# A two-layer trunk whose first projection takes its inputs in another order: loads of both token halves in one transfer, memory keys block by block, and the memory's scale factor spread later

## The chip, the core and the metric

The kernel runs on one core of a Trainium2 chip. The engines spoken of are TensorE (PE: matrix products, with weight loads listed apart as PEld), VectorE (DVE), ScalarE (ACT), GpSimd (POOL) and SyncE (SP, which here only issues transfers). The metric is the device time of one execution in microseconds (us), as the median of several runs.

## The reference

What is computed is a trunk of two layers of width 2048 for 256 tokens, each layer with a mixer, an attention into 256 memory tokens and a gated feed-forward part. All inputs are float32. Cut to what matters here (the mixers and the feed-forward part are left in words, since the change lies ahead of them):

```python
def rmsnorm(x, g):
    y = x * rsqrt(mean(x * x, axis=-1, keepdims=True) + EPS)
    return y * g

def memory_attention(q_m, mem, g_mem, w_mem_kv):       # 4 heads of 128
    q = q_m.reshape(B, S, 4, 128)
    kv = rmsnorm(mem, g_mem) @ w_mem_kv                # (256 x 2048) @ (2048 x 1024)
    k, v = kv[..., :512] , kv[..., 512:]               # each as (B, 256, 4, 128)
    s = einsum('bshd,bmhd->bhsm', q, k) * 128 ** -0.5
    return einsum('bhsm,bmhd->bshd', softmax(s), v).reshape(B, S, 512)

for l in range(2):
    h = rmsnorm(x, g_mix[l])
    if l == 0: main, q_m = spatial gating of h @ w_in_a
    else:      main, q_m = latent attention of h @ w_in_b over keys from layer 0's result
    mo = memory_attention(q_m, mem, g_mem[l], w_mem_kv[l])
    x = x + concatenate([main, mo]) @ w_out[l]
    x = x + conv_ffn(rmsnorm(x, g_ffn[l]), w_ffn_up[l], conv_w[l], conv_b[l], w_ffn_down[l])
return rmsnorm(x, g_final)
```

The memory's keys and values of both layers depend on `mem`, `g_mem` and `w_mem_kv` alone, not on `x`. So the kernel can compute them first, while `x` is still on its way.

## The kernel before, in words

**Products.** Partitions are P = 128 rows; D = 2048 is NB = 16 blocks of 128. A float32 product is made of three products of reduced operands: each operand is split into a high part and a low part, and the kernel adds hi x hi, hi x lo and lo x hi. `chunk` (L98) loads two blocks of weights, 128 x 1024 elements (512 KB), into a tile `raw` of which there are four. Where a norm's gain has to be applied (it does for the memory's weights), ACT writes `whi` for each block as a scaled copy (L121) and DVE writes `wlo`, the scaled weights less `whi` (L122). `whi` and `wlo` have five tiles each.

`gemm_fm` (L161) leaves the features of the result on the partitions; its inner loop `mm_fm` (L152) runs, for a chunk of two input blocks and four output blocks, first all products with `whi` (L155 with the operand's high part, L156 with its low part, alternating), then all with `wlo` (L158), 24 products of 256 columns. `gemm_tm` (L199) leaves the tokens on the partitions (L193 to L195, 512 columns each). Four accumulators in PSUM stay open over all 16 input blocks.

**The start.** `start` (L433) makes, in this order, the memory's keys of layer 0 (`gemm_fm`), its values (`gemm_tm`), the keys of layer 1 and the values of layer 1. The memory tokens come as they lie, a token on a partition, in two tiles `mtok` of 128 tokens each, and must be transposed: `token_transpose` (L398) puts two blocks of both halves through PE (L403, four transposes, one group in what follows), then `put_mem` (L449) has ACT write the high part `memhl` (L452) and DVE the low part (L453). `token_load` (L393) loads a range of columns, with one transfer for each half. `gains` (L315) loads rows of gains, transposes them on PE (L327) and has DVE copy them to `gT` (L328); without `gT` no memory weight can be split.

`begin` (L487) holds what comes ahead of the first product. It spreads the first transfers over the queues of ACT and SP: quarters of the first four blocks of tokens (128 rows x 256 columns each), the weights of blocks 0 and 1 as two halves of one `raw`, and the gains. Between, `idle` (L481) lets PE multiply ones by ones, 11 times in all, the results of which nothing reads. Token blocks 0 and 1 are transposed before `gemm_fm` is entered, blocks 2 and 3 after the first chunk's split.

**What sets the order.** The keys of layer 0 stand in a region in which the order on ACT, DVE, PE and SP is the order of the program (`manual_schedule`). There `gemm_fm` splits chunk n+1 before it multiplies chunk n (L176 to L183), and the hooks in `first` put, after the products of chunk c, the transposes of blocks 2c+4 and 2c+5 and the loads of the later tokens. What follows the region is put in order by a scheduler; the program gives it hooks too, which run after a given chunk. In the hooks of the layer-0 values stand the loads of x, the memory's squares on ACT (L412), their sums, and in the one of chunk 5 `scale_keys` (L469). `scale_keys` spreads the memory's factor, 1/rms of each memory token, over all partitions: `spread` (L423) has DVE multiply the identity by the factor (`diag`, L428) and PE multiply ones by it (L429), once for each half; ACT copies the sum, and POOL multiplies layer 0's four key tiles by it (L472). The keys of layer 1 are multiplied by the same spread factor when they are evicted.

Of the kernel before, what the change touches and what calls it, by code (L numbers as in the profile page):

```python
# [69 lines left out]
class Kernel:  # L70
# [27 lines left out]
    def chunk(self, src, nk, ncol, gains=None, heads=None, raw=None, moves=False):  # L98
        nc, n = self.nc, nk * ncol
        loaded = raw is not None  # L100
        if not loaded:
            raw = self.wp.tile([P, 1024], F32, tag="raw", name=self.uid("raw"), bufs=4)
        hi, lo = self.split_tile("whi", moves), self.split_tile("wlo", moves)
        view = lambda x: x[:, :n].rearrange("p (k c) -> p k c", k=nk)
        if not loaded:
            nc.sync.dma_start(out=view(raw), in_=src)
# [54 lines left out]
    def gemm_fm(self, src, kbs, nblk, rhs, evict, nk=2, gain=None, hooks={}, raw=None):  # L161
# [3 lines left out]
        def split(c):  # L165
            g = None if gain is None else [gain(kbs[c + i]) for i in range(nk)]
            hi, lo = self.chunk(src(kbs[c], nk), nk, nblk * P, g, raw=raw if c == 0 else None)
# [8 lines left out]
        ready = []  # L176
        for n, c in enumerate(chunks):
            ahead = chunks[n : n + 2] if raw is not None else [c]
            for d in ahead[len(ready) :]:
                ready.append(split(d))  # L180
                for f in hooks.get(-1, ()) if d == 0 else ():
                    f()
            self.mm_fm(ready.pop(0))  # L183
            for f in hooks.get(n, ()):
                f()
# [207 lines left out]
    def token_load(self, src, tok, k0, k1):  # L393
        c = slice(k0 * P, k1 * P)
        for tb in range(2):
            self.nc.sync.dma_start(out=tok[tb][:, c], in_=src[tb * P : (tb + 1) * P, c])

    def token_transpose(self, tok, k0, k1, put):  # L398
        for k in range(k0, k1, 2):
            acc = self.psum()  # L400
            for i in range(2):
                for tb in range(2):
                    self.nc.tensor.transpose(  # L403
                        acc[:, i * S + tb * P : i * S + (tb + 1) * P], tok[tb][:, (k + i) * P : (k + i + 1) * P], self.ident
                    )
# [3 lines left out]
    def token_squares(self, tok, part, j, pool):  # L409
        for tb in range(2):  # L410
            junk = self.tmp(pool, [P, 512], "junk", 2)
            ins = self.nc.scalar.activation(  # L412
                junk, tok[tb][:, j * 512 : (j + 1) * 512], AF.Square, accum_out=part[:, tb, j : j + 1]
# [19 lines left out]
    def start(self):  # L433
# [8 lines left out]
        with tc.tile_pool(name="st", bufs=1) as st:  # L442
            self.gp = st
            mtok = [st.tile([P, D], F32, name=f"mtok{tb}") for tb in range(2)]
            xtok = [st.tile([P, D], F32, name=f"xtok{tb}") for tb in range(2)]
# [28 lines left out]
            raw = self.wp.tile([P, 1024], F32, tag="raw", name=self.uid("raw"), bufs=4)  # L474
            first = {c: [mturn(2 * c + 4, 2 * c + 6)] for c in range(-1, 6)}
            first[-1].append(lambda: idle(1))
            for c, piece in ((0, (4, 6)), (1, (6, 8)), (2, (8, 12)), (4, (12, 16))):
                first[c].insert(0, mload(*piece))


# [618 lines left out]
```

## Time and profile before

| | |
|---|---|
| median of 3 runs | 2065.43 us (2065.27 to 2065.58) |
| the profiled execution | 2065.32 us |
| its span in the profile | 2063.6 us |
| PE busy in the span | 2053.1 us (99%) |
| ACT busy | 1074.8 us (52%) |
| DVE busy | 1376.3 us (67%) |
| moved by DMA | 392.56 MB, mean 190 GB/s |
| first product of the keys of layer 0 | at 8.63 us |
| first product of the values of layer 0 | at 34.17 us |

The profile is one execution. Times in its rows count from the start of the span; the execution's time includes about 1.7 us around it. A row of the timeline names the start, the duration, the engine, the line of the kernel, the operation and its tiles (written <- read), and in brackets the idle time before it with what ended it. The waits view sums idle time by the instruction that waited and what released it. Matmuls overlap, so two rows that start 0.114 us apart may each be listed with 0.28 us; what PE takes is read from the distance of starts.

### The profile page before, as it was taken

The numbers are of one execution on the slowest core, as the hardware profiler recorded it, in microseconds if no ns is written. First come the engines' busy times: TensorE is split into PE (matmuls) and PEld (weight loads), VectorE is DVE, ScalarE is ACT, GpSimd is POOL, SyncE is SP. The second block draws the span as 40 slices with busy tenths as digits, with TensorE's granted clock in tenths as the row PEclk, the third lists the DMA queues.
The fourth block names the chain that finished last, engine by engine and source line by source line (L and its number), as shares of the span: only waits on it lengthen the run. The fifth ranks groups of instructions, "written<-read, shape, count | busy, mean of one in ns | idle before, by whom it ended". The sixth has DMA issues, their size and how long they took to land.

```text
span 2063.6 us, 39742 instructions
## 1 busy us (share of the span) xinstructions
PE 2053.1 (99%) x16322; PEld 1984.5 (96%) x16322; DVE 1376.3 (67%) x2051; ACT 1074.8 (52%) x1536; POOL 141.2 (7%) x200
## 2 busy tenths in 40 slices
PE   9999999999999999999999999999999999999998
PEld 9889999999999999999999999999988999889996
DVE  5656666776656767557788676776765677646765
ACT  6754644555534555345555574455543555435554
POOL 0000012100000000000043241400000000000000
PEclk9999999999999999999999999999999999999999
DMA  8665556566556665566555634565655666556654
GB/s 271 207 214 174 163 186 200 187 197 193 195 194 194 194 194 194 194 194 195 194 194 175 184 122 165 184 204 181 192 191 193 196 197 194 191 194 195 195 183 143
DMA packets 208122, 392.56 MB, mean 190 GB/s; under 512 B 14334, under 2 KB 23876, under 8 KB 207812
## 3 DMA queue, kind: packets, MB, share of 16 engines
q1 hardware_dynamic: 207364, 388.98, 58.2%
q8 instruction: 127, 2.08, 0.4%
q10 hardware_dynamic: 576, 1.05, 0.2%
q14 instruction: 55, 0.45, 0.1%
HBM read 387.88 MB, written 2.10 MB: 189 GB/s over the span
## 4 chain that ended last, share of the span: by engine, by line
PE 97%; DMA 1%; ACT 1%; DVE 0%; issue 0%; SPq 0%; ACTq 0%; DVEq 0%
PE ps L155 26%; PE ps L156 26%; PE ps L158 26%; PE ps L193 6%; PE ps L194 6%; PE ps L195 6%; DMA raw<-in_w_mem_kv 1%; ACT whi L121 0%; PE ps L918 0%; PE ps L919 0%; PE ps L581 0%; PE ps L546 0%; DMA xtok<-in_x 0%; PE ps L729 0%; PE ps L952 0%
## 5 line engine op out<-in xcount | busy, mean ns | idle before, releaser
L117 DVE TENSOR_TENSOR wlo<-raw,whi 128x1024 fp32r<-128x1024 f32 x660 | 818.6, 1243 | 543.9 <-ACT whi L116 537.6
L116 ACT ACTIVATE whi<-raw 128x1024 fp32r<-128x1024 f32 x660 | 701.1, 1063 | 868.1 <-PE ps L156 664.7
L155 PE MATMUL ps<-xhl,whi 128*128 128x256 f32 x3264 | 764.6, 277 | 0.0
L156 PE MATMUL ps<-xhl,whi 128*128 128x256 f32 x3264 | 761.1, 276 | 0.0
L156 PEld LDWEIGHTS ps<-xhl,whi 128*128 128x128 f32 x3264 | 612.9, 188 | 0.5
L155 PEld LDWEIGHTS ps<-xhl,whi 128*128 128x128 f32 x3264 | 612.7, 188 | 0.5
L158 PE MATMUL ps<-xhl,wlo 128*128 128x256 f32 x3264 | 437.0, 276 | 0.0
L158 PEld LDWEIGHTS ps<-xhl,wlo 128*128 128x128 f32 x3264 | 400.6, 188 | 0.0
L155 PE MATMUL ps<-h,whi 128*128 128x256 f32 x704 | 163.6, 276 | 0.0
L156 PE MATMUL ps<-h,whi 128*128 128x256 f32 x704 | 163.6, 276 | 0.0
L194 PE MATMUL ps<-wlo,h 128*128 128x512 f32 x354 | 137.3, 388 | 0.0
L193 PE MATMUL ps<-whi,h 128*128 128x512 f32 x354 | 137.3, 388 | 0.0
L195 PE MATMUL ps<-whi,h 128*128 128x512 f32 x354 | 137.0, 388 | 0.0
L156 PEld LDWEIGHTS ps<-h,whi 128*128 128x128 f32 x704 | 132.0, 188 | 0.0
L155 PEld LDWEIGHTS ps<-h,whi 128*128 128x128 f32 x704 | 131.8, 188 | 0.0
L155 PE MATMUL ps<-mainhl,whi 128*128 128x256 f32 x512 | 119.7, 277 | 0.0
L156 PE MATMUL ps<-mainhl,whi 128*128 128x256 f32 x512 | 119.6, 276 | 0.0
L634 ACT ACTIVATE c<-a,cT 128x256 f32<-128x256 f32 x176 | 99.5, 589 | 0.0
L122 DVE SCALAR_TENSOR_TENSOR wlo<-raw,gT,whi 128x512 fp32r<-128x512 f32 x112 | 83.9, 788 | 20.0 <-ACT whi L121 17.1
L156 PEld LDWEIGHTS ps<-mainhl,whi 128*128 128x128 f32 x512 | 96.1, 188 | 0.0
L155 PEld LDWEIGHTS ps<-mainhl,whi 128*128 128x128 f32 x512 | 96.1, 188 | 0.0
L158 PE MATMUL ps<-h,wlo 128*128 128x256 f32 x704 | 94.1, 276 | 0.0
(266 smaller groups left out, 2205.3 us busy)
## 6 DMA issues: line engine op xcount, KB each, us to landing
raw<-in_w_ffn_up SPq DMA_DIRECT2D x352, 512.0 KB, 3.5
raw<-in_w_ffn_down SPq DMA_DIRECT2D x176, 512.0 KB, 4.0
raw<-in_w_out SPq DMA_DIRECT2D x64, 512.0 KB, 4.5
raw<-in_w_in_a SPq DMA_DIRECT2D x56, 512.0 KB, 3.7
raw<-in_w_mem_kv SPq DMA_DIRECT2D x31, 512.0 KB, 4.9
raw<-in_w_in_b SPq DMA_DIRECT2D x16, 512.0 KB, 4.2
raw<-in_w_kv_a SPq DMA_DIRECT2D x9, 512.0 KB, 4.1
raw<-in_w_uq SPq DMA_DIRECT2D x12, 384.0 KB, 3.5
```

What stands on the lines that cost most here:

```text
L116: nc.scalar.activation(hi[:, :n], raw[:, :n], AF.Copy)
L117: nc.vector.tensor_tensor(lo[:, :n], raw[:, :n], hi[:, :n].bitcast(F32), ALU.subtract)
L122: nc.vector.scalar_tensor_tensor(lo[:, s], raw[:, s], gains[k], hi[:, s].bitcast(F32), ALU.mult, ALU.subtract)
L155: mm(acc[:, :S], wh, x[:, :S], start=first, stop=False)
L156: mm(acc[:, :S], wh, x[:, S:], start=False, stop=False)
L158: mm(acc[:, :S], wl, x[:, :S], start=False, stop=last)
L193: mm(acc, xh, wh, start=first, stop=False)
L194: mm(acc, xh, wl, start=False, stop=False)
L195: mm(acc, xl, wh, start=False, stop=last)
L634: nc.scalar.activation(c, a, AF.Identity, scale=w(2), bias=w(3))
```

## The change

- `token_load` takes both halves of the tokens in one transfer (128 partitions x 2 halves x the columns); `mtok` and `xtok` become one tile each, `[P, 2, D]`. The memory's tokens come in five transfers (before, twelve), those of x in four (eight).
- `first_keys` replaces `begin` and the call of `gemm_fm` for layer 0. It multiplies block by block, 12 products each: four hi x hi, four with `wlo`, four hi x lo. After the products of block k come, in program order, the load of a weight chunk, a load of tokens, a transpose group where `turns` has one, and the split of block k+2. Seven groups stand between products and one ahead of the first (before, six and two).
- The first transfers: gains, weights of block 0 and tokens of blocks 2 and 3 from ACT's queue; tokens of blocks 0 and 1, weights of block 1, then the chunks from SP's. The first `whi` stands on ACT ahead of the copy of the first transpose group.
- `idle` runs 8 products in all, not 11.
- `gains` is cut in two (`gain_load`, `gain_turn`), so that the load can be issued earlier than the transpose.
- `scale_keys` goes from the hook of chunk 5 of the layer-0 values to that of chunk 1 of the layer-1 keys. On PE the first of its products stood after the last product of the layer-0 values and now stands after the second chunk of the layer-1 keys.

The parts of `chunk` and `gemm_fm` that took a loaded `raw` and split one chunk ahead are removed, as nothing uses them now; for the other calls they do the same. The core of the diff:

```diff
     def gains(self, names):
-        nc, t = self.nc, self.t
+        self.gain_turn(self.gain_load(names, self.nc.sync))
+
+    def gain_load(self, names, queue):
+        t = self.t
         raw = self.tmp(self.gp, [P, P], "graw", 2)
         r = 0
         for name in names:
             src = t[name] if len(t[name].shape) == 1 else t[name].rearrange("l d -> (l d)")
             src = src.rearrange("(k p) -> k p", p=P)
             n = src.shape[0]
-            nc.sync.dma_start(out=raw[r : r + n, :], in_=src)
+            queue.dma_start(out=raw[r : r + n, :], in_=src)
             self.g[name] = self.ng + r
             r += n
+        return raw, r
+
+    def gain_turn(self, rows):
+        nc, (raw, r) = self.nc, rows
         acc = self.psum()
         nc.tensor.transpose(acc[:, :r], raw[:r, :], self.ident[:r, :r])
         nc.vector.tensor_copy(self.gT[:, self.ng : self.ng + r], acc[:, :r])
...
     def token_load(self, src, tok, k0, k1):
         c = slice(k0 * P, k1 * P)
-        for tb in range(2):
-            self.nc.sync.dma_start(out=tok[tb][:, c], in_=src[tb * P : (tb + 1) * P, c])
+        self.nc.sync.dma_start(out=tok[:, :, c], in_=src.rearrange("(a p) c -> p a c", p=P)[:, :, c])
...
-            mtok = [st.tile([P, D], F32, name=f"mtok{tb}") for tb in range(2)]
-            xtok = [st.tile([P, D], F32, name=f"xtok{tb}") for tb in range(2)]
+            mtok = st.tile([P, 2, D], F32, name="mtok")
+            xtok = st.tile([P, 2, D], F32, name="xtok")
...
-            def begin():
-                src = self.rows(t["w_mem_kv"][0], 0, MW)(0, 2)
-                piece = lambda q, k0, tb: q.dma_start(
-                    out=mtok[tb][:, k0 * P : (k0 + 2) * P], in_=t["mem"][0][tb * P : (tb + 1) * P, k0 * P : (k0 + 2) * P]
-                )
-                weights = lambda q, k: q.dma_start(out=raw[:, k * MW : (k + 1) * MW], in_=src[:, k, :])
-                piece(nc.scalar, 0, 1)
-                weights(nc.scalar, 0)
-                idle(4)
-                self.gains(("g_mem",))
-                piece(nc.sync, 0, 0)
-                weights(nc.sync, 1)
-                piece(nc.scalar, 2, 0)
-                piece(nc.sync, 2, 1)
+            def first_keys(evict):
+                src = self.rows(t["w_mem_kv"][0], 0, MW)
+                mem = t["mem"][0].rearrange("(a p) c -> p a c", p=P)
+                accs = [self.psum() for _ in range(MH)]
+                chunks = []
+
+                def tokens(queue, k0, k1):
+                    c = slice(k0 * P, k1 * P)
+                    queue.dma_start(out=mtok[:, :, c], in_=mem[:, :, c])
+
+                def weights(*queues):
+                    raw = self.wp.tile([P, 1024], F32, tag="raw", name=self.uid("raw"), bufs=4)
+                    n = 2 // len(queues)
+                    for i, queue in enumerate(queues):
+                        view = raw[:, i * n * MW : (i + 1) * n * MW].rearrange("p (k c) -> p k c", k=n)
+                        queue.dma_start(out=view, in_=src(2 * len(chunks) + i * n, n))
+                    chunks.append([raw])
+
+                def split(k):
+                    ch, c, g = chunks[k // 2], slice(k % 2 * MW, (k % 2 + 1) * MW), self.gain("g_mem", k)
+                    if k % 2 == 0:
+                        ch += [self.split_tile("whi"), self.split_tile("wlo")]
+                    raw, hi, lo = ch
+                    nc.scalar.activation(hi[:, c], raw[:, c], AF.Copy, scale=g)
+                    nc.vector.scalar_tensor_tensor(lo[:, c], raw[:, c], g, hi[:, c].bitcast(F32), ALU.mult, ALU.subtract)
+
+                def products(k):
+                    _, hi, lo = chunks[k // 2]
+                    for n, (w, x) in enumerate(((hi, mhl[:, k, :S]), (lo, mhl[:, k, :S]), (hi, mhl[:, k, S:]))):
+                        for b, acc in enumerate(accs):
+                            o = k % 2 * MW + b * P
+                            nc.tensor.matmul(
+                                acc[:, :S], w[:, o : o + P], x, start=k == 0 and n == 0, stop=k == NB - 1 and n == 2
+                            )
+
+                turn = lambda k: self.token_transpose(mtok, k, k + 2, put_mem)
+                gain_rows = self.gain_load(("g_mem",), nc.scalar)
+                tokens(nc.sync, 0, 2)
+                weights(nc.scalar, nc.sync)
+                tokens(nc.scalar, 2, 4)
+                weights(nc.sync)
                 idle(5)
-                mturn(0, 2)()
+                self.gain_turn(gain_rows)
+                tokens(nc.sync, 4, 8)
+                weights(nc.sync)
+                split(0)
+                idle(2)
+                turn(0)
                 idle(1)
+                split(1)
+                turns = {0: 2, 2: 4, 3: 6, 5: 8, 7: 10, 9: 12, 11: 14}
+                for k in range(NB):
+                    products(k)
+                    if k % 2 == 0 and len(chunks) < NB // 2:
+                        weights(nc.sync)
+                    if k in (0, 2):
+                        tokens(nc.sync, 2 * k + 8, 2 * k + 12)
+                    if k in turns:
+                        turn(turns[k])
+                    if k + 2 < NB:
+                        split(k + 2)
+                for b, acc in enumerate(accs):
+                    evict(b, acc)
             hooks = [
-                first,
+                None,
                 {
                     0: [lambda: self.gains(("g_mix", "g_ffn", "g_kv")), xload(0, 4), msq(0), msq(1)], 1: [xload(4, 8), msq(2), msq(3)],
                     2: [lambda: self.token_rstd(mpart, st, mrt), xload(8, 12)], 3: [xload(12, 16), xturn(0, 4)], 4: [self.masks],
-                    5: [scale_keys], 6: [lambda: self.gains(("g_v", "g_kv_lat", "g_q_lat"))],
+                    6: [lambda: self.gains(("g_v", "g_kv_lat", "g_q_lat"))],
                 },
-                {0: [xturn(4, 8)], 2: [xturn(8, 12)], 4: [xturn(12, 16)], 6: [xsq(0)]},
+                {0: [xturn(4, 8)], 1: [scale_keys], 2: [xturn(8, 12)], 4: [xturn(12, 16)], 6: [xsq(0)]},
                 {
                     0: [xsq(1)], 1: [xsq(2)], 2: [xsq(3), lambda: self.conv_consts(0)], 3: [lambda: self.token_rstd(xpart, st, self.rt)],
                     5: [lambda: self.spread(self.rb, self.rt), lambda: self.conv_consts(1)],
...
                 ET = mybir.EngineType
                 with tc.manual_schedule(engines={ET.Activation, ET.DVE, ET.PE, ET.SP}) if l == 0 else nullcontext():
                     if l == 0:
-                        begin()
-                    self.gemm_fm(
-                        self.rows(w, 0, MW), list(range(NB)), MH, m, ek, gain=g, hooks=hooks[2 * l], raw=raw if l == 0 else None
-                    )
+                        first_keys(ek)
+                    else:
+                        self.gemm_fm(self.rows(w, 0, MW), list(range(NB)), MH, m, ek, gain=g, hooks=hooks[2])
                 self.gemm_tm(self.rows(w, MW, MW), NB, MW, m, ev, gain=g, hooks=hooks[2 * l + 1])
```

More of the change, by code (lines that the diff above doesn't have):

```diff
@@ L95, in split_tile, with chunk @@
         return w[:, :1024] if moves else w[:, 19 : 19 + 1024]
[L98 removed]
+    def chunk(self, src, nk, ncol, gains=None, heads=None, moves=False):
         nc, n = self.nc, nk * ncol
[L100 to L102 removed]
+        raw = self.wp.tile([P, 1024], F32, tag="raw", name=self.uid("raw"), bufs=4)
         hi, lo = self.split_tile("whi", moves), self.split_tile("wlo", moves)
         view = lambda x: x[:, :n].rearrange("p (k c) -> p k c", k=nk)
[L105 to L106 removed]
+        nc.sync.dma_start(out=view(raw), in_=src)
         if heads is not None:
@@ L166, in split @@
             g = None if gain is None else [gain(kbs[c + i]) for i in range(nk)]
-            hi, lo = self.chunk(src(kbs[c], nk), nk, nblk * P, g, raw=raw if c == 0 else None)
+            hi, lo = self.chunk(src(kbs[c], nk), nk, nblk * P, g)
             jobs = []
@@ L174, in split @@
             return jobs
-        ready = []
         for n, c in enumerate(chunks):
[L178 to L183, printed above, removed]
+            self.mm_fm(split(c))
             for f in hooks.get(n, ()):
```

12 lines of the change are left out of this document (4 added, 8 removed).

## The prediction

> **What bounds the kernel now.** I read the page's sums first, then the waits of TensorE, then the timeline of the first 60 us.
>
> ```profile
> span 2063.6 us, 39742 instructions
> ...
> PE 2053.1 (99%) x16322; PEld 1984.5 (96%) x16322; DVE 1376.3 (67%) x2051; ACT 1074.8 (52%) x1536; POOL 141.2 (7%) x200
> ```
>
> TensorE (PE) is busy 2053.1 of 2063.6 us. The change moves nothing later than the layer-1 keys, so only the first 80 us can gain or lose. A stall of PE there costs its length, since PE works through without a pause; the longest of its few waits in that stretch are these:
>
> ```profile
> PE ps L484 <- DVE ones L292: 1.1, 1, 1.1
> PE ps L429 <- DVE diag L428: 0.8, 1, 0.8
> ```
>
> Columns: sum, count, mean. The first lies ahead of the first product, where PE only idles or transposes. The 0.8 us on the factor's diagonal is inside the work. So three places count: when the first product can start, what PE loses between there and the end of the layer-0 keys, and the diagonal. In the timeline rows below the columns are start, duration, engine, line, operation; the bracket is the idle time before and its releaser.
>
> ```profile
> 2.21 1.28 ACT L452 ACT_TABLE_LOAD   x1 [2.21 <-issue]
> 4.02 0.19 DVE L328 COPY gT<-ps 128x32 f32<-128x32 f32 x1 [2.96 <-PE ps L327]
> 7.30 0.60 ACT L452 ACTIVATE memhl<-ps 128x512 fp32r<-128x512 f32 x1 [3.81 <-PE ps L403]
> 7.80 1.33 ACT L121 ACTIVATE whi<-raw,gT 128x512 fp32r<-128x512 f32 x2
> 8.63 0.56 PE L155 MATMUL ps<-memhl,whi 128*128 128x256 f32 x1
> ...
> 34.17 0.40 PE L193 MATMUL ps<-whi,memhl 128*128 128x512 f32 x1
> ```
>
> The first product starts at 8.63, released by the first `whi`, behind the token transpose's copy (7.30). ScalarE (ACT) stood idle 3.81 us for that transpose. The key products end at the first value product, 34.17.
>
> **The change part by part.** I add the terms to the profiled execution, 2065.32 us for its 2063.6 us of span; the median of the three runs, 2065.43, is 0.11 above it.
>
> *1. First product, -1.5 us.* Now `whi` of block 0 is made before the token transpose is waited for. But the order on ACT is new too: its table load, free at 2.21 in the shadow of the transfers, now stands behind the wait for raw block 0, since `whi` is the first ACTIVATE. When does block 0 land? 16 KB of gains, 256 KB of tokens and 256 KB of weights go first, 0.54 MB.
>
> ```profile
> 1.00:2.00 1.00, 0.88 (x4) 0.88 (x5) 0.06 (x1) 0.00 (x0) 0.96 (x6) 1.00 0.06 20
> 2.00:3.00 1.00, 1.00 (x6) 0.90 (x5) 0.00 (x0) 0.79 (x1) 0.22 (x1) 1.00 0.71 180
> 3.00:4.00 1.00, 0.49 (x3) 0.26 (x2) 0.00 (x0) 0.50 (x1) 0.00 (x0) 1.00 0.84 306
> raw<-in_w_mem_kv SPq DMA_DIRECT2D x31, 512.0 KB, 4.9
> ```
>
> In the windows the last column is GB/s, in the transfer row it is the median from issue to landing. 20 + 180 + 306 KB gives 0.506 MB by 4.00, so 0.54 MB is reached near 4.2. That is the lower bound; transfers issued behind these share the bandwidth, and the median of 4.9 us, counted from 1.0 where the first bytes move, would give 5.9. I take 4.5, near the lower bound because the byte counts come from this very stage. Then 1.28 us of table load, 0.61 for `whi` (two take 1.33, a second one 0.72, rows above and below), 0.60 for the token copy and 0.11 from there to PE (8.52 to 8.63): 4.5 + 1.28 + 0.61 + 0.60 + 0.11 = 7.1. Against 8.63 that is -1.5; bounds -1.8 and -0.1. The gains (`gT`) were there at 4.21 in the old order; their load is now the first on its queue, so they come no later. The idle products, 11 before and 8 now, stand in time in which PE waits either way: nothing.
>
> *2. The slow clock, +0.7 us.* Products before 10.1 are slow:
>
> ```profile
> 9.77 0.41 PE L155 MATMUL ps<-memhl,whi 128*128 128x256 f32 x1
> 9.99 0.35 PE L156 MATMUL ps<-memhl,whi 128*128 128x256 f32 x1
> 10.17 0.28 PE L155 MATMUL ps<-memhl,whi 128*128 128x256 f32 x1
> 10.29 0.28 PE L156 MATMUL ps<-memhl,whi 128*128 128x256 f32 x1
> ```
>
> The distance between starts drops from 0.22 to 0.12 (0.114 over the eight products between 13.24 and 14.15 below), although the clock column of the windows reads 1.00. If the switch stays at 10.1, the 1.53 us between 7.1 and 8.63 do only 0.114 / 0.22 = 0.52 of a fast stretch's work: 1.53 x 0.48 = 0.7 lost. Bounds: -0.7 (switch before 7.1, so that the slow 1.47 us of the old kernel go too) and +2.1 (3.0 us later); see the rivals.
>
> *3. One more transpose group among the products, +0.4 us.* Blocks 2 and 3 were transposed before the first product; now they follow products of block 0. A group holds PE for 0.36 us in the old kernel (12.33 to 12.69 in the rows of the next term), and I add 0.09 for the restart of products that reading a new operand shows there (13.24 - 12.69 is 0.55, four distances of 0.114 are 0.46).
>
> *4. Waits after each transpose group, +3.2 us.* This is the largest term. Before, PE had a whole chunk, 24 products, between a transpose group and the products whose split ACT made behind that group; now it has one block, 12. After a transpose group ACT must first copy the group (`memhl`) and then make `whi` of the block two on, and DVE the same with the low parts. In the loop the order is: products(k), transposes, products(k+1), products(k+2); products(k+2) need what ACT starts only when the transposes end. In the gap PE has only products(k+1):
>
> ```profile
> 12.33 0.60 PE L403 MATMUL ps<-ident,mtok 128*128 128x128 f32 x4
> 12.69 0.36 PE L155 MATMUL ps<-memhl,whi 128*128 128x256 f32 x1
> ...
> 13.24 0.28 PE L155 MATMUL ps<-memhl,whi 128*128 128x256 f32 x1
> ...
> 14.15 0.28 PE L155 MATMUL ps<-memhl,whi 128*128 128x256 f32 x1
> ```
>
> From the first product after a group (12.69) to the thirteenth (14.15) it is 1.46 us; the first four take 0.55 (to 13.24). ACT and DVE in the same stretch:
>
> ```profile
> 12.97 0.60 ACT L452 ACTIVATE memhl<-ps 128x512 fp32r<-128x512 f32 x1 [2.13 <-PE ps L403]
> 13.46 0.72 ACT L121 ACTIVATE whi<-raw,gT 128x512 fp32r<-128x512 f32 x1
> 13.60 0.69 DVE L453 TENSOR_TENSOR memhl<-ps,memhl 128x512 fp32r<-128x512 f32 x1 [1.71 <-ACT memhl L452]
> 14.21 0.75 DVE L122 SCALAR_TENSOR_TENSOR wlo<-raw,gT,whi 128x512 fp32r<-128x512 f32 x1
> ```
>
> ACT begins its copy 0.28 after 12.69, has `whi` at 13.46 + 0.72 = 14.18, and PE sees it 0.11 later: 1.60 against 1.46, so PE is 0.14 late. Four products on hi·xh follow (0.55). The next four need `wlo`, done at 14.21 + 0.75 = 14.96, seen at 2.27 + 0.11 = 2.38 after 12.69; PE is there at 1.60 + 0.55 = 2.15, again 0.23 late. Two restarts cost about 0.09 each. So 0.14 + 0.23 + 0.18 = 0.55 per group. There are seven groups: those behind blocks 0, 5, 7, 9 and 11 take the whole (2.8 us), the one behind 3 about 0.4 since ACT is ahead there, the one behind 2 nothing: 3.2. Lower bound nothing, if ACT gains lead over the products between groups; upper bound 7 x 0.55 = 3.9.
>
> *5. The factor's spread, -0.95 us.* Its two diagonals move from the end of the layer-0 values into the second chunk of the layer-1 keys.
>
> ```profile
> 56.74 0.39 PE L195 MATMUL ps<-whi,memhl 128*128 128x512 f32 x1
> 57.58 0.28 DVE L428 TENSOR_SCALAR diag<-ident,mrt 128x128 f32<-128x128 f32 x1
> 57.92 0.38 PE L429 MATMUL ps<-diag,ones 128*128 128x128 f32 x1 [0.79 <-DVE diag L428]
> ```
>
> PE's last value product starts at 56.74 and occupies 0.23 (its neighbours' distance), so PE is free at 56.97 and starts at 57.92: 0.95 lost. Two diagonals, two small products, one copy and four POOL multiplications all remain, so nothing else falls away. Moved later, DVE's diagonal lies among the chunk's splits whose sums are long done; the first reader of the spread factor, the eviction of the layer-1 keys, comes six chunks after it, and the scaled keys are read only in layer 0's attention. What is late next at 56.97 is `whi` of the first layer-1 chunk. ACT is the full engine between 35 and 57, but without the diagonal PE reaches this point no sooner than the keys' stage allows, and the value stage starts later by term 4, which leaves ACT more lead. Bounds -0.95 and 0.
>
> *6. Loads merged.* Twelve token transfers on the memory side become five, eight of x become four; each row still moves the same bytes. Each issue is a fraction of a us on SP or ACT, which are not late. I take nothing; the bad end is a rival (D).
>
> Sum: -1.5 + 0.7 + 0.4 + 3.2 - 0.95 = +1.85. 2065.32 + 1.85 = 2067.17; with the 0.11, **2067.3 us**, that is +0.09%.
>
> **The rivals.**
>
> *B. The order hides the waits.* Term 4 is nothing, because ACT and DVE get ahead by a whole group in the nine blocks without a transpose. For it: a block takes PE 1.4 us and ACT 0.72. Against: rows 12.69 to 14.96 chain directly. Gives -1.35: 2064.1; with the first product 0.4 sooner, 2063.7.
>
> *C. The switch of the clock moves.* It may follow what PE did before, not a fixed time. In the old kernel products had run 1.47 us, 8.63 to 10.1. Counted so, the switch comes at 8.6 here and term 2 is nothing (C'): 2066.6. If transposes and waits, of which there are now more, hold it up by as much as twice that, 3.0 us, it costs another 3.0 x 0.48 = 1.4 and takes 0.5 off the waits, as a slow PE waits less (C): 2068.2. The only rows that bear on it are the switch between 9.99 and 10.17. [...]
>
> *D. Transfers of x stand in front of weights (the other side: slower).* In the new queue the first three x transfers, 0.5 MB each, come ahead of weight chunk 5; before, chunk 5 was ahead of them. Chunk 5 is needed near 26.2, six blocks of 1.46 and two groups with their waits, 1.0 each, ahead of the keys' end (34.17 - 1.5 + 0.7 + 0.4 + 3.2 = 36.9). 7.4 MB lie before and in it.
>
> ```profile
> 0.00:7.00 7.00, 5.38 (x23) 5.05 (x24) 0.36 (x2) 1.28 (x1) 1.59 (x10) 1.00 0.67 188
> 7.00:14.00 7.00, 7.00 (x49) 6.91 (x48) 4.35 (x7) 4.56 (x8) 0.00 (x0) 1.00 1.05 384
> 14.00:21.00 7.00, 7.00 (x64) 7.00 (x63) 4.69 (x8) 4.28 (x8) 0.00 (x0) 1.00 1.00 308
> 21.00:28.00 7.00, 7.00 (x64) 7.00 (x63) 4.67 (x8) 3.81 (x7) 0.00 (x0) 1.00 0.91 338
> 28.00:35.00 7.00, 7.00 (x62) 6.87 (x62) 3.84 (x6) 4.39 (x9) 0.00 (x0) 1.00 0.70 217
> ```
>
> At these rates 7 x 188 KB are 1.3 MB by 7.0 and 2.7 MB more by 14.0; the 3.4 MB left take 7 us at 308 (2.16 MB) and 3.7 at 338: 24.7, in time by 1.5. The first x transfer comes up after 3.7 MB, near 13.2. If x goes at the lowest row's 217 GB/s from there, the remaining 3.7 MB take 17 us, chunk 5 lands at 30.2, and PE stands 4.0 us: 2071.3. It decides under 3.7 MB / 13.0 us = 285 GB/s, and is measurable under 3.7 / 15.3 = 242.
>
> *E. The table load holds up the start.* If it needs as much more behind the wait as lies between my landing and the late bound, 1.4 us, the first product comes at 8.5, term 1 is -0.1 and term 2 nothing: 2067.9. The trace speaks against it:
>
> ```profile
> 50.94 1.37 ACT L121 ACTIVATE whi<-raw,gT 128x512 fp32r<-128x512 f32 x2
> 52.32 1.28 ACT L265 ACT_TABLE_LOAD   x1
> ```
>
> The load follows the ACTIVATE at once and takes 1.28. [...]
>
> **How the numbers follow.** Chances: forecast 0.47 (2067.3), B 0.20 (2064.1), C 0.11 (2068.2), C' 0.08 (2066.6), D 0.09 (2071.3), E 0.05 (2067.9). A measurement of this kernel can tell about 0.2%, 4.1 us: faster means below 2061.3, slower above 2069.6. No case reaches 2061.3; 0.02 is left for a first product and waits both better than all bounds. Slower is D and a little of C's upper end, 0.10. The rest, 0.88, is the same. The range goes from B's lower end, 2063.7, to 2069.6, below D; about 0.15 is left out. Within it the cases divide on the sign: B is faster, A, C and E are slower, all by less than can be told; the forecast's own range is 2066.0 (waits at half) to 2068.0.
>
> **What would show it.** Right: the first product near 7.1 with the table load just behind the landing of block 0 and ahead of the first `whi`; slow distances until 10.1; gaps of 0.1 to 0.3 us of PE on `whi` and on `wlo` in each second block after a transpose group; the first value product near 36.9 (34.17 before); no wait on the diagonal. Wrong: PE without gaps between 10 and 35 (B), distances of 0.21 after 10.3 (C), a wait on raw of 2 us or more near block 10 (D), a first product after 8.3 (E or a late landing).

## The result and the profile after

| | before | after |
|---|---|---|
| median | 2065.31 us (16 runs, 2064.28 to 2066.57) | 2069.39 us (16 runs, 2068.57 to 2071.05) |
| ratio | | 1.0020, 95% interval [1.0012, 1.0028] |
| profiled execution, span | 2065.32, 2063.6 us | 2069.05, 2067.3 us |
| PE busy | 2053.1 us | 2054.9 us |

The changed kernel is 4.1 us slower, where I had forecast 1.9 us. That is outside the forecast's own range (2066.0 to 2068.0) and only 0.2 us inside the upper end of the wide one, the line that I had drawn between the same and slower. The page's first rows and all waits of PE in the first 100 us of the kernel after:

```profile
span 2067.3 us, 39720 instructions
...
PE 2054.9 (99%) x16316; PEld 1984.5 (96%) x16316; DVE 1375.7 (67%) x2051; ACT 1074.6 (52%) x1536; POOL 141.0 (7%) x200
```

```profile
PE ps L508 <- ACT memhl L449: 2.9, 1, 2.9
PE ps L474 <- DVE ones L283: 1.1, 1, 1.1
```

PE now stands 2.9 us in one piece ahead of the first product, which the kernel before did not. The wait on the diagonal is gone. The timeline of ACT and PE shows what PE waited for:

```profile
5.52 0.39 PE L474 MATMUL ps<-ones 128*128 128x128 f32 x2
8.79 1.22 PE L508 MATMUL ps<-memhl,whi 128*128 128x256 f32 x4 [2.88 <-ACT memhl L449]
```

```profile
6.24 1.28 ACT L500 ACT_TABLE_LOAD   x1 [6.24 <-DMA raw<-in_w_mem_kv]
7.54 0.72 ACT L500 ACTIVATE whi<-raw,gT 128x512 fp32r<-128x512 f32 x1
8.16 0.58 ACT L449 ACTIVATE memhl<-ps 128x512 fp32r<-128x512 f32 x1
```

ACT waits to 6.24 for block 0's weights, then come the table load, `whi` and the token copy in the order that I had written down, 2.55 us from the landing to the first product (forecast 2.60). The tokens were transposed long before (4.85 to 5.52). The clock is in the windows of the same kernel (columns: stretch, length, busy time of PE, PEld, DVE, ACT and POOL with the instructions begun, PE's granted clock, DMA share, GB/s):

```profile
8.00:9.00 1.00, 0.21 (x1) 0.21 (x2) 0.71 (x2) 1.00 (x3) 0.00 (x0) 0.87 1.04 354
9.00:10.00 1.00, 1.00 (x5) 1.00 (x6) 1.00 (x3) 0.35 (x1) 0.00 (x0) 0.50 1.01 385
10.00:11.00 1.00, 1.00 (x7) 1.00 (x6) 0.30 (x1) 0.00 (x0) 0.00 (x0) 0.50 1.04 403
11.00:12.00 1.00, 1.00 (x7) 1.00 (x6) 0.00 (x0) 0.00 (x0) 0.00 (x0) 0.50 1.07 410
12.00:13.00 1.00, 1.00 (x10) 1.00 (x9) 0.00 (x0) 0.53 (x2) 0.00 (x0) 0.93 1.07 370
```

0.87 is 0.26 us at half speed, so the clock closed at 8.74; 0.93 is 0.14 us, so it opened at 12.14. The first 3.4 us of products run at half speed. From then on, each stretch behind a transpose group looks like the first of these, to the last:

```profile
13.19 1.28 PE L508 MATMUL ps<-memhl,whi 128*128 128x256 f32 x8
14.52 0.73 PE L508 MATMUL ps<-memhl,wlo 128*128 128x256 f32 x4
15.09 0.62 PE L508 MATMUL ps<-memhl,whi 128*128 128x256 f32 x4
15.54 0.60 PE L400 MATMUL ps<-ident,mtok 128*128 128x128 f32 x4
15.90 0.72 PE L508 MATMUL ps<-memhl,whi 128*128 128x256 f32 x4
16.46 0.62 PE L508 MATMUL ps<-memhl,wlo 128*128 128x256 f32 x4
...
33.65 1.26 PE L508 MATMUL ps<-memhl,whi 128*128 128x256 f32 x8
34.97 0.75 PE L508 MATMUL ps<-memhl,wlo 128*128 128x256 f32 x4
35.55 1.09 PE L508 MATMUL ps<-memhl,whi 128*128 128x256 f32 x8
...
37.84 0.62 PE L184 MATMUL ps<-whi,memhl 128*128 128x512 f32 x2
```

Eight products of 0.114 are 0.91, but the `wlo` products start 1.33 after them, and these four take 0.57 in place of 0.46: 0.42 + 0.11 = 0.53 us, split into pauses so short that the waits view does not list them. Six of the seven groups have it (the rows x8 at 13.19, 18.80, 22.48, 26.24, 29.95 and 33.65), with 0.48 to 0.54 us each, 3.1 together. So a ledger from the two profiles: start 8.79 - 8.63 = +0.16; half speed for 3.36 us of products in place of 1.47, (3.36 - 1.47) x 0.48 = +0.9; one more group +0.46 (0.36 from 15.54 to 15.90, and 0.10 for the restart, as the four products behind it take 0.56 in place of 0.46); waits +3.1: the keys end 4.6 us later. (Eight of their products lie behind the first value product here, so that 37.84 shows only 3.7 of it.) 0.95 comes back at the diagonal: +3.7, the difference of the spans. The medians lie 0.4 us further apart than these two executions, which is less than the executions of one kernel differ.

### The profile page after: what moved, and what is told of

Read it like the earlier page. It is cut to its first block, busy times and chain, and to the rows that moved or that the text cites. A ratio compares the mean times of both kernels' runs of the same rounds, so it can differ in the third digit from the quotient of the medians.

```text
span 2067.3 us, 39720 instructions
## 1 busy us (share of the span) xinstructions
PE 2054.9 (99%) x16316; PEld 1984.5 (96%) x16316; DVE 1375.7 (67%) x2051; ACT 1074.6 (52%) x1536; POOL 141.0 (7%) x200
## 3 DMA queue, kind: packets, MB, share of 16 engines
q10 hardware_dynamic: 608, 1.07, 0.1%
## 4 chain that ended last, share of the span: by engine, by line
PE 99%; DVE 0%; ACT 0%; DMA 0%; issue 0%; ACTq 0%
PE ps L152 26%; PE ps L153 26%; PE ps L155 26%; PE ps L184 6%; PE ps L185 6%; PE ps L186 6%; PE ps L508 1%; PE ps L953 0%; PE ps L954 0%; PE ps L616 0%; PE ps L400 0%; PE ps L581 0%; PE ps L764 0%; PE ps L987 0%; DMA raw<-in_w_mem_kv 0%; DVE wlo L501 0%
## 5 line engine op out<-in xcount | busy, mean ns | idle before, releaser
L232 DVE TENSOR_TENSOR a<-ps,rbc 128x256 f32<-128x256 f32 x176 | 69.9, 418 | 27.7 <-PE ps L155 27.7
```

The source lines that it names most:

```text
L232: self.nc.vector.tensor_tensor(out, acc[:, :S], r, ALU.mult)
```

## The experiments

Each run was timed against the kernel before in its own session; ratio and interval stand with each. The intervals are some 0.09% to either side, 1.8 us, so the differences between variants are read from the medians of 11 runs together with the trace of each. "Half speed" is read from the distances of products, 0.21 us in place of 0.114.

**e1_lo_last.** Part of the waits: `wlo` needed last.

```diff
-((hi, mhl[:, k, :S]), (lo, mhl[:, k, :S]), (hi, mhl[:, k, S:]))
+((hi, mhl[:, k, :S]), (hi, mhl[:, k, S:]), (lo, mhl[:, k, :S]))
```

> The changed kernel with the order of each block's 12 products turned to hi x hi, hi x lo of the tokens, then the four that need wlo. Theory: of the 3.1 us that PE loses after six transpose groups, the part on wlo (0.22 + 0.11 us at 14.19 and 14.52, and so in each group, 6 x 0.33 = 2.0 us) goes, as wlo is needed 0.45 us later; the 0.2 us on whi stays: 2069.4 - 2.0 = 2067.4. Rival: ACT and DVE as a whole are too slow for a block of 1.4 us, the lateness only moves to the next block: 2069.4.

Measured: 2067.34, ratio 1.0011 [1.0003, 1.0020], 2.05 us under the changed kernel. The share on `wlo`, which I had sized at 0.33 us for each of six groups, is real and goes when its reader comes 0.45 us later.

**e2_split_first.** All the waits: the split ahead of the transposes.

```diff
-                    if k in turns:
-                        turn(turns[k])
                     if k + 2 < NB:
                         split(k + 2)
+                    if k in turns:
+                        turn(turns[k])
```

> The changed kernel with split(k + 2) ahead of the transpose group in the program, so that ACT and DVE make whi and wlo of block k+2 before they wait for the transposes. Theory: all waits after the groups go, 3.1 us: 2069.4 - 3.1 = 2066.3, the first product stays at 8.8. Rival: the copy of the tokens (memhl) comes too late instead, at the group behind block 0 above all, and at least 0.3 us for each group stays: 2067.5 or more.

Measured: 2066.39, ratio 1.0006 [0.9997, 1.0015], 3.0 us under the changed kernel, as the theory gave. Its trace has no pause between 14 and 35 us. It is the most costly single part of the change, and it is the order of two statements. The profile of this run shows products at half speed until 14, in its windows:

```profile
12.00:13.00 1.00, 1.00 (x7) 1.00 (x6) 0.03 (x1) 0.66 (x2) 0.00 (x0) 1.00 1.08 397
13.00:14.00 1.00, 1.00 (x6) 1.00 (x6) 1.00 (x2) 1.00 (x2) 0.00 (x0) 1.00 1.04 337
14.00:15.00 1.00, 1.00 (x11) 1.00 (x10) 1.00 (x2) 0.16 (x1) 0.00 (x0) 1.00 1.06 372
```

PE issues 6 or 7 products in a microsecond before 14 and 11 after, and the clock column reads 1.00 all the while.

**e3_table_early.** The table load out of the chain.

```diff
+                early = st.tile([P, 1], F32, name="early")
+                nc.scalar.activation(early, self.ones[:, :1], AF.Copy)
                 idle(5)
                 self.gain_turn(gain_rows)
```

> The changed kernel with one small ACT copy of a column of ones (result read by nothing) ahead of the first whi, so that the table load no longer waits for block 0's weights. Theory: the table load lies near 2.3, whi starts when block 0 has landed (6.2), the first product comes near 7.6 in place of 8.8. If the switch of the clock stays near 12.1, half of that is lost again to slow products: 2069.4 - 0.6 = 2068.8; if the switch follows PE's start: 2069.4 - 1.2 = 2068.2. Rival: something other than the table load (the token copy, the gains) holds the first product: 2069.4.

Measured: 2067.87, ratio 1.0013 [1.0003, 1.0022], 1.5 us under the changed kernel. ACT's timeline of this run:

```profile
2.29 1.28 ACT L519 ACT_TABLE_LOAD   x1 [2.29 <-issue]
3.58 0.20 ACT L519 ACTIVATE early<-ones 128x1 f32<-128x1 f32 x1
6.73 0.72 ACT L500 ACTIVATE whi<-raw,gT 128x512 fp32r<-128x512 f32 x1 [2.95 <-DMA raw<-in_w_mem_kv]
```

```profile
7.99 0.75 PE L508 MATMUL ps<-memhl,whi 128*128 128x256 f32 x4 [1.79 <-ACT memhl L449]
```

The load is back in the shadow of the transfers. `whi` starts as soon as block 0 has landed, here 6.73, later than in the changed kernel's own profile, so only 0.8 of the 1.28 show in this execution's first product (7.99). PE's pause ahead of it is down to 1.8 us, but the clock still closes:

```profile
9.00:10.00 1.00, 1.00 (x9) 1.00 (x8) 0.50 (x1) 0.00 (x0) 0.00 (x0) 0.70 1.04 363
...
12.00:13.00 1.00, 1.00 (x7) 1.00 (x7) 1.00 (x2) 0.48 (x1) 0.00 (x0) 0.60 1.08 386
```

0.70 and 0.60 give 9.40 to 12.80, again 3.4 us, at another time than 8.74 to 12.14. The profile of e1, where PE paused for 2.5 us, has a third closure:

```profile
9.00:10.00 1.00, 0.91 (x5) 0.63 (x5) 1.00 (x2) 0.15 (x1) 0.00 (x0) 0.55 1.02 393
...
12.00:13.00 1.00, 1.00 (x8) 1.00 (x8) 0.00 (x0) 0.54 (x2) 0.00 (x0) 0.75 1.07 392
```

0.55 and 0.75 give 9.10 to 12.50. So the length is the same each time, and the time does not follow PE's first product (8.79, 8.59 in e1, 7.99). My two prices for this run took the time as fixed (2068.8) or tied to PE's start (2068.2); neither was right, and 2067.87 does not tell them apart.

**e4_spread_only.** The move of `scale_keys` alone, on the kernel before.

```diff
-                    5: [scale_keys], 6: [lambda: self.gains(("g_v", "g_kv_lat", "g_q_lat"))],
+                    6: [lambda: self.gains(("g_v", "g_kv_lat", "g_q_lat"))],
-                {0: [xturn(4, 8)], 2: [xturn(8, 12)], 4: [xturn(12, 16)], 6: [xsq(0)]},
+                {0: [xturn(4, 8)], 1: [scale_keys], 2: [xturn(8, 12)], 4: [xturn(12, 16)], 6: [xsq(0)]},
```

> The kernel before with scale_keys moved alone. Theory: the 0.95 us that PE lost on the diagonal goes and nothing takes its place: 2065.3 - 0.95 = 2064.4. Rival: the split of the first chunk of the layer-1 keys is as late as the diagonal was and PE waits for it: 2065.3.

Measured: 2064.30 against 2065.37, ratio 0.9996 [0.9987, 1.0005]: 1.07 us less by the medians; the interval takes in no difference at all. No wait of PE is left in its values. The trace shows the wait gone; that the 1.07 is this wait is argued and not shown, since e7 below comes out as far down with the diagonal's place unchanged.

**e5_fill.** The pause of PE filled, nothing else sooner.

```diff
                 turn(0)
-                idle(1)
+                idle(7)
```

> The changed kernel with seven idle products in place of one between the first transpose group and the first product, so that PE does not stand for 2.9 us (5.9 to 8.8); nothing else is changed, and the first product may come up to 0.2 us later. Theory: it is the pause that closes the clock for a window of 3.41 us (0.50 from 8.73 to 12.15 in the clock rows); without it the clock stays open once it has opened, some 3 us of products at half speed become fast, and the time falls by about 1.4: 2068.0. Rival: the clock closes or opens late for another reason (the transposes, or nothing but the phase): 2069.4 or a little more.

Measured: 2067.62, ratio 1.0011 [1.0003, 1.0020], 1.8 us under the changed kernel although nothing that is used comes sooner (first product 8.85). Its windows:

```profile
8.00:9.00 1.00, 0.15 (x1) 0.15 (x2) 0.65 (x1) 1.00 (x3) 0.00 (x0) 1.00 1.03 359
9.00:10.00 1.00, 1.00 (x10) 1.00 (x11) 1.00 (x3) 0.41 (x1) 0.00 (x0) 1.00 1.02 383
10.00:11.00 1.00, 1.00 (x11) 1.00 (x10) 0.36 (x1) 0.03 (x1) 0.00 (x0) 1.00 1.06 410
```

Ten or eleven products in a microsecond from the start, where the changed kernel had 5 to 7. A pause of 1.2 us is still there and does no harm. So PE's pause of 2.9 us costs some 1.8 us besides its own length: in the changed kernel the clock closes behind it (0.50 from 8.74 to 12.14), and the products start at half speed; here the column reads 1.00 from 7 to 13. (In the profile of e2, with a pause of 1.8 us, PE begins 6 to 8 instructions in each microsecond from 9 to 14 and 11 from 14 to 15, and the column reads 1.00 all the while; I read that as a clock that had not opened yet and opened late.) How long a pause has to be for that is not shown: 2.9 us were enough in the profile of the changed kernel, 2.5 in that of e1 and 1.8 in that of e3, and the 1.2 us here were not.

**e6_k0_first.** Block 0's weights ahead of the gains on ACT's queue; the gains go to SP's.

```diff
-                gain_rows = self.gain_load(("g_mem",), nc.scalar)
+                gain_rows = self.gain_load(("g_mem",), nc.sync)
```

> The changed kernel with the first two issues exchanged between the queues: block 0's weights are now the first transfer on ACT's queue, the gains the first on SP's, so block 1's weights come one place later behind the tokens. Theory: block 0 landed at 6.2 because block 1's weights were issued beside it and shared the bytes; now it lands near 4.4 and the first product comes 1.8 us sooner, near 7.0: between 2067.6 (clock stays open) and 2068.5 (half of it lost to a closed clock). Rival: the landing is set by something other than the bytes ahead of it: 2069.4.

Measured: 2067.30, ratio 1.0009 [1.0000, 1.0018], 2.1 us under the changed kernel. ACT and PE in its timeline:

```profile
3.79 1.28 ACT L500 ACT_TABLE_LOAD   x1 [3.79 <-DMA raw<-in_w_mem_kv]
...
6.83 0.60 ACT L449 ACTIVATE memhl<-ps 128x512 fp32r<-128x512 f32 x1 [1.03 <-PE ps L400]
```

```profile
5.68 1.11 PE L400 MATMUL ps<-ident,mtok 128*128 128x128 f32 x4 [0.67 <-DMA mtok<-in_mem]
...
7.48 0.79 PE L508 MATMUL ps<-memhl,whi 128*128 128x256 f32 x2 [0.26 <-ACT memhl L449]
```

Block 0 lands at 3.79 in place of 6.24: one place in the queues is 2.45 us, of which the earlier issue (0.80, before 1.29) makes 0.5. The run moves the gains, the tokens and block 1's weights too, so it does not tell which neighbour had cost how much. Then the tokens are the last to land (5.68) and the first product comes at 7.48, 0.5 later than I had set. What is behind the first transfers does matter: as block 0 lands sooner (3.79, before 6.24), the first tokens land later (5.68, in the changed kernel by 4.85). The time falls by more than the 1.3 us of the first product; PE's pause has also shrunk, to 0.7 and 0.3 us, and e5 puts a price on that.

**e7_loads_only.** The merged loads alone, on the kernel before, with `begin` as it was.

```diff
-        for tb in range(2):
-            self.nc.sync.dma_start(out=tok[tb][:, c], in_=src[tb * P : (tb + 1) * P, c])
+        self.nc.sync.dma_start(out=tok[:, :, c], in_=src.rearrange("(a p) c -> p a c", p=P)[:, :, c])
...
-            mtok = [st.tile([P, D], F32, name=f"mtok{tb}") for tb in range(2)]
-            xtok = [st.tile([P, D], F32, name=f"xtok{tb}") for tb in range(2)]
+            mtok = st.tile([P, 2, D], F32, name="mtok")
+            xtok = st.tile([P, 2, D], F32, name="xtok")
```

> The kernel before with the tokens of both halves in one tile and the later loads of memory tokens and of x merged into one transfer each; the first four quarter loads and all orders as before. Theory: nothing, 2065.3. Rival: x's transfers, now fewer and sooner in the queue than weights, make a chunk of weights late by 1 us or more: 2066.3 or more.

Measured: 2064.37 against 2065.33, ratio 0.9996 [0.9987, 1.0004]. The merged loads do no harm; that they help by 1 us isn't shown. In its one profile the clock happens to be open at the first product (8.66; products are 0.12 apart from 8.86), and PE has pauses of 0.4 us and less near 24 and 28.5 that the kernel before does not have, and none on the diagonal. What remains of the 0.96 us by medians is open.

**e8_all.** The mends of e2, e3 and e6 together, and `idle(2)` ahead of the first product in place of `idle(1)`; the diffs are those above.

> The changed kernel with all mends: split(k + 2) ahead of the transposes, table load early, block 0's weights first on their queue, one more idle product. Theory: first product near 6.4 to 6.6 in place of 8.8, no waits after transpose groups, no diagonal, clock open at a time that its phase sets and not closed again: against the kernel before -2.2 for the start, +0.5 for more products at half speed, +0.45 for one more group, -0.95 for the diagonal: 2063.1. Rival: the sooner start is lost to slow products and to transfers that cannot keep up (block 1 or chunk 1 late), so that only the diagonal is left as a gain: 2064.4 or more.

Measured: 2065.53, ratio 1.0002 [0.9993, 1.0010]. A miss by 2.4 us. Its waits of PE:

```profile
PE ps L400 <- DMA mtok<-in_mem: 1.5, 1, 1.5
PE ps L474 <- DVE ones L283: 1.1, 1, 1.1
PE ps L508 <- ACT whi L500: 0.6, 1, 0.6
```

The first tokens landed last (the first product at 8.32), and near 25.4 PE waited for `whi` of a block whose weights had been issued behind x. That is rival D of the prediction, on a smaller scale: a PE that is 3.5 us sooner there (the sixth transpose group among the products at 25.10, 28.58 in the changed kernel) meets the transfers that a late one never saw. PE begins 7 instructions from 9 to 10 and 11 from 10 to 11, so fast products start near 10, as in the kernel before; that a phase sets this time is not shown.

**e9_all_x_late.** As e8, with tokens of blocks 2 and 3 behind block 1's weights on SP's queue, and x behind the layer-0 keys' last weights.

```diff
-                tokens(nc.scalar, 2, 4)
+                tokens(nc.sync, 2, 4)
...
+                for k in range(0, NB, 4):
+                    xload(k, k + 4)()
                 for b, acc in enumerate(accs):
                     evict(b, acc)
```

The four `xload` are taken out of the hooks.

> The kernel of the run before with all mends, with two more: tokens of blocks 2 and 3 go behind block 1's weights on SP's queue, so that tokens 0 and 1 share the bytes with block 0's weights alone, and x's four transfers come behind the last weight chunk of the layer-0 keys. Theory: what that run lost was a wait of 1.5 us on the first tokens and 1.1 us on chunk 5 behind x; with both gone the first product comes near 6.2 and PE has no gap to the values: 2065.5 - 2.3 = 2063.2, less if part of the sooner start is at half speed. Rival: the late x makes the first value chunks or the transposes of x late by as much: 2065.0 or more.

Measured: 2063.50 against 2065.63, ratio 0.9989 [0.9980, 0.9998]. 0.3 us over the theory, and under both kernels. First product at 6.46. One wait has moved to the values:

```profile
PE ps L184 <- ACT whi L118: 1.2, 1, 1.2
PE ps L474 <- DVE ones L283: 1.1, 1, 1.1
PE ps L508 <- ACT memhl L449: 0.7, 2, 0.4
```

**e10_before_few_idle.** The kernel before with one idle product for each call of `idle`.

```diff
-                for _ in range(n):
+                for _ in range(min(n, 1)):
```

> The kernel before with each call of idle cut to one product (11 products in all become 4), so that PE stands some 2 us more before the first product; nothing waits for the idle products. Theory: the pause keeps the clock closed for one more window of 3.41 us in most executions, so 1.5 us or more of products at half speed are added: 2066.5 to 2067.0. Rival: idle products do nothing for the clock: 2065.3.

Measured: 2065.62 against 2065.63, ratio 1.0001 [0.9992, 1.0010]: the rival's time, but not for the rival's reason. From its PE timeline:

```profile
8.91 0.56 PE L155 MATMUL ps<-memhl,whi 128*128 128x256 f32 x1
...
10.76 0.41 PE L155 MATMUL ps<-memhl,whi 128*128 128x256 f32 x1
10.97 0.41 PE L156 MATMUL ps<-memhl,whi 128*128 128x256 f32 x1
```

```profile
57.47 0.40 PE L195 MATMUL ps<-whi,memhl 128*128 128x512 f32 x1
57.70 0.39 PE L429 MATMUL ps<-diag,ones 128*128 128x128 f32 x2
```

The start is 0.3 us later and products are still 0.21 apart at 10.97 (fast from 10.17 before); one profile does not tell whether that comes from the fewer idle products, as the profile of e4, with all of them, also differs from the kernel before (products near 0.12 apart from 8.62). That a pause ahead of the first product adds 3.41 us at half speed is not shown. PE is 0.73 us later at the last value product (57.47, before 56.74). But then it goes straight on to the diagonal, 0.23 later, where it had waited 0.95. So in the kernel before some 0.9 us of any delay ahead of 57 us are free, as PE is waiting for ACT and DVE there.

**e11_spread_back.** The changed kernel with `scale_keys` where it was (the reverse of the diff of e4).

> The changed kernel with scale_keys back in the hook of chunk 5 of the layer-0 values. If the terms add up as I added them, the 0.95 us on the diagonal comes back: 2069.4 + 0.95 = 2070.3. Rival: in the changed kernel the values start 3.7 us later on PE while ACT and DVE are not later by as much, so the diagonal is ready in time anyway and moving it was worth nothing on top of the rest: 2069.4.

Measured: 2069.28, ratio 1.0017 [1.0009, 1.0026], the rival's. From its DVE and its PE timeline:

```profile
59.29 0.29 DVE L425 TENSOR_SCALAR diag<-ident,mrt 128x128 f32<-128x128 f32 x1
```

```profile
62.16 0.39 PE L426 MATMUL ps<-diag,ones 128*128 128x128 f32 x2
```

The diagonal is ready 2.6 us before PE comes. In the changed kernel the move is worth nothing: the late keys had used up what it could give.

**e12_all_x_between.** As e9, but x behind the first four chunks of the layer-0 values, with SP in program order there.

```diff
-                self.gemm_tm(self.rows(w, MW, MW), NB, MW, m, ev, gain=g, hooks=hooks[2 * l + 1])
+                with tc.manual_schedule(engines={ET.SP}) if l == 0 else nullcontext():
+                    self.gemm_tm(self.rows(w, MW, MW), NB, MW, m, ev, gain=g, hooks=hooks[2 * l + 1])
```

The four `xload` are back in the hooks of chunks 0 to 3.

> The kernel of the run before last with all mends and x late (2063.5), but with x's four transfers behind the first, second, third and fourth weight chunk of the layer-0 values, one each, the order on SP's queue being that of the program for these values. Theory: the 1.3 us that PE waited for the first value chunk (32.18, its weights behind 2 MB of x) go: 2063.5 - 1.3 = 2062.2. Rival: the values are bound by ACT and DVE in any case, which stand ahead of PE only by what PE waits here, so that the wait comes back later in the values: 2063.5.

Measured: 2062.55 (2062.32 to 2062.77) against 2065.15, ratio 0.9987 [0.9978, 0.9996]. It beats both kernels, by 2.6 and 6.8 us by the medians. Its waits of PE in the first 100 us and its first product:

```profile
PE ps L474 <- DVE ones L283: 1.1, 1, 1.1
```

```profile
6.55 1.22 PE L508 MATMUL ps<-memhl,whi 128*128 128x256 f32 x4
```

Nothing is waited for after the first product.

## Why the prediction was right or wrong, point by point

The direction and the largest term were right, the sum was 2.2 us short. The step that failed is in the first term: "I take 4.5, near the lower bound" for the landing of block 0's weights. It makes 1.7 us of the 2.2; the clock makes 0.2, and the rest is what the medians differ beyond the profiled executions.

1. *First product, -1.5 us forecast, +0.16 measured.* The chain after the landing was right to 0.05 us. The landing was 6.24, later even than my late bound of 5.9, and my own sign of it, a first product after 8.3, came (8.79). I had counted the bytes ahead of block 0, 0.54 MB, and set what is issued beside it down as a small share. But block 1's weights go out beside it on SP's queue, with the tokens of blocks 2 and 3 half a microsecond behind, and chunk 1 too. The windows up to the landing, of the changed kernel and of e6, say what that takes:

```profile
1.00:6.24 5.24, 4.79 (x21) 4.27 (x21) 0.25 (x2) 0.00 (x0) 1.17 (x6) 1.00 0.77 238
```

```profile
1.00:3.79 2.79, 2.67 (x11) 2.39 (x11) 0.06 (x1) 0.01 (x1) 1.18 (x6) 1.00 0.56 180
```

5.24 x 238 KB = 1.25 MB had moved when block 0 landed in the changed kernel; in e6, with block 0 one place sooner, it was 2.79 x 180 KB = 0.50 MB, at 3.79. How the queues share the DMA engines is not shown; the landings and the bytes moved by them are. The table load in the chain was foreseen and costs as set (1.28 us at 6.24; e3: 1.5 us with what hangs on it).
2. *The slow clock, +0.7 forecast, about +0.9 in the profiles.* The number is near, the mechanism was not there. I had one switch, from slow to fast, at a time that might move. In the changed kernel the clock closes again behind PE's pause of 2.9 us (0.50 from 8.74 to 12.14), and filling the pause gives back 1.8 us (e5), where the 3.36 us at half speed cost 3.36 x 0.48 = 1.6 in the profile. So the late start cost twice. C came near in size for another reason: not transposes and short waits, but one long pause.
3. *One more group, +0.4:* +0.46, restart included.
4. *Waits after each transpose group, +3.2:* 3.1 in the profile; 3.0 undone by e2, 2.0 of it by e1. The split between `whi` (0.2) and `wlo` (0.33) was 0.23 and 0.32 in my working, restarts counted. I had five full groups and one at 0.4; it is six full ones. B is refuted.
5. *The diagonal, -0.95.* It is gone and the ledger needs the -0.95, but it does not come from the move. I had added the terms as if they were independent. Whatever makes the keys late by more than 0.95 removes that wait by itself (e11: 0.1 us between with and without), and e10 shows the same slack in the kernel before. The move alone is worth some 1 us by the medians (e4, not clear of the noise), on top of a late first projection nothing.
6. *Loads merged, nothing:* nothing bad shown (e7). D, with 4 us, did not come in the changed kernel; it came with 0.6 us of wait on `whi` in e8, when PE was early enough to meet it, and went with x moved (e9, e12). E's start near 8.5 came, but not from the table load, which took 1.28.

What stays open: the 0.96 us of e7 by medians; which of block 0's neighbours in the queues cost how much; and what decides whether a pause closes the clock (1.2 us did not in the one profile of e5, 1.8, 2.5 and 2.9 did), its length alone or also when it falls.

## What to carry to other kernels

Block 0's weights landed at 6.24 us, with 1.25 MB moved, behind the gains on ACT's queue, and at 3.79, with 0.50 MB moved, as the first on it (e6): put what is needed first at the head of its queue, with nothing beside it that can wait. A sum of terms holds only where no slack lies between them: look for the next wait downstream, since it takes back a delay up to its own length, and a gain too (here 0.95 us, e10 and e11). When two engines pass work to a third in program order, put the piece that waits for nothing ahead of the piece that waits (3.0 us in e2).

## What the runs showed of the hardware

- Behind a pause of PE of 2.9, 2.5 and 1.8 us the clock closed, to 0.50, for 3.4 us (8.74 to 12.14 in the changed kernel, 9.10 to 12.50 in e1, 9.40 to 12.80 in e3); behind a pause of 1.2 us in the same place (e5) it did not.
- When the clock first opens differs between executions of the same code: up to the values e4 is the kernel before, and its products are 0.12 apart almost from the first, at 8.42, where the profile of the kernel before has 0.22 until 10.1.
- The clock column of the windows reads 1.00 also at the start, while products are 0.22 us apart (until 10.1 in the kernel before) or PE begins 6 or 7 in a microsecond (from 12 to 14 in e2, 11 from 14 to 15). There "half speed" is a reading of the distances, which the column does not show.
- ACT's table load stood behind the wait for the transfer that the first ACTIVATE reads: it waited to 6.24 for block 0's weights, in e6 to 3.79, and a copy of one column ahead, which reads no weights, moved it to 2.29 (e3). In the kernel before, where the first ACTIVATE reads what PE had transposed, at 7.30, the load did not wait for that and stood at 2.21.
